# A layer kernel's attention stage: later value products, division moved to the output projection, maxima moved by transfers, loads moved to SyncE

## The chip, the cores and the metric

The kernel runs on one core of a Trainium2 chip, in one launch. The metric is the device time of that launch in microseconds. Before the change it is 2820.78 us, the median of three runs (2816.55 to 2822.61). Inputs and outputs are fp32.

## What is computed

One layer of a streaming encoder, for a prompt of 2048 frames and for eight streams of 16 new frames with 1024 cached frames each. Width 1024; half of the mixer is a convolution module of 512 channels, half is attention with 8 heads of 64. Cut to what matters:

```python
sh1, sc1, g1, sh2, sc2, g2 = split(silu(c) @ w_ada + b_ada)
h = rmsnorm(x, norm1_g) * (1 + sc1) + sh1
u_a, u_g, q, k, v, f = split(h @ w_in)
u = u_a * sigmoid(u_g)
q, k = rmsnorm(q, q_norm_g), rmsnorm(k, k_norm_g)        # per head
logf = log_sigmoid(f + b_f)
s = q @ k.T * 64 ** -0.5 + (cum_q[:, None] - cum_k[None, :])   # cum = cumsum(logf)
attn = softmax(where(k_pos <= q_pos, s, -1e30)) @ v
conv = silu(layernorm(depthwise_conv31(u) + conv_b) * ln_g + ln_b)
x = x + g1 * (concat(conv, attn) @ w_out)
h = rmsnorm(x, norm2_g) * (1 + sc2) + sh2
x = x + g2 * ((silu(h @ w_gate) * (h @ w_up)) @ w_down)
```

The outputs are x, the new keys, values, log forget values and convolution states.

## The kernel before, in words

fp32 products on TensorE are made of two parts: each operand is split into a rounded high part (a copy on ScalarE) and a low part (a subtraction on VectorE or GpSimd, `parts_of`, L1158), and a product is three matmuls: high by high, low by high, high by low.

The stages follow each other: the input projection of the gate, values and forget logits (`project_u_v`), queries and keys (`project_q_k`), attention (`attention`, L778), the output projection (`project_out`, L1178), and the feed-forward network (`ffn_up`, `ffn_down`). The depthwise convolution runs on VectorE beside the projections.

Attention over the prompt goes through 16 steps, `STEPS`: for each of four pairs of heads p, four blocks qb of 512 queries. A step has 8(qb + 1) pieces: for each block of 128 keys and each head of the pair a score product of 128 keys by up to 512 queries (`attend`, L954). A piece takes: two score matmuls (L973 with the keys' high and low parts, L977 with the rest of the operand), on the diagonal a third that adds the mask (L979); the exponential on ScalarE (L981); the split of its result into two parts `e` (L1160 and L1161, every third subtraction on GpSimd); and three value matmuls (L964) into one of two PSUM banks per head, `pv`. The value operand has a block of ones between the two heads' columns, so that the sums of the exponentials come out of the same products. Pieces wait in the list `waiting` and two are taken off it when it is too long; what is left at the end of the step is emptied there.

The softmax subtracts a maximum over keys. It is not found from the scores themselves: a separate product of the high parts (L934, with a mask at L936) gives approximate scores with queries on the partitions, VectorE reduces them (L937), and the result of a step is transposed on TensorE (L948) and written into 8 rows of the query operand `Q2` (L950), where a constant block mask `bm` puts each of the 8 values (head and block of 128 queries) into its own row and columns; rows of minus one in the key operand then subtract it within the score product. The maxima run ahead of the scores by `AHEAD` and `LEAD` pieces, and L974 orders a first score behind a maxima product further on.

Loads for attention: keys (L889, L891) and queries (L903, L927) are started from GpSimd's queue, values (L906) from SyncE's. There are six buffers for key blocks, four for `Q2`, two for `Q1`.

At the end of a step (L995 to L1006) ScalarE copies sums and values out of the two banks (four copies of 64 partitions), makes the reciprocal with Ln and Exp, VectorE refines it and multiplies (L1003 to L1005), and a DMA stores the block to `cat_d` in HBM, from which the output projection reads.

Beside the steps runs `background`: the norm of the convolution's output (`conv_norm`, five chunks, with two Newton rounds, L92, for an inverse root), then the attention of the eight streams (`sample_setup`, `sample_batch`), all through one PSUM bank `lane`. `weave` deals out turns of the steps, the maxima, the loads and the background by count; `nback` is the background's number of turns. A planner (`schedule_with_timeline_sim`) then sets the order on every engine and queue from priorities and its own estimate of times; `after` adds an order between two instructions of one engine without a semaphore.

The output projection takes six blocks of 360 or 368 frames (`HALVES`). In each it goes through eight chunks of 128 input channels, attention's four first (`OUT_ORDER`); it loads a chunk from `cat_d` (L1196), splits it and adds 24 matmuls into 8 accumulators, one PSUM bank each (L1144). Then each accumulator is scaled and added to x (L1152) in a buffer `x`, of which there are 20, and stored. The buffers of blocks 0 and 1 are kept for the second norm, which follows block 2 (L1226); those of later blocks come free when they are stored and squared.

## Time and profile before

The profile is of one execution, on the one core.

| what | us |
|---|---|
| runs, median (lowest to highest) | 2820.78 (2816.55 to 2822.61) |
| the profiled execution's own time | 2814.3 |
| its span, first to last instruction | 2812.5 |
| busy in the span: TensorE matmuls | 2718.6 |
| busy: VectorE / ScalarE / GpSimd | 2161.9 / 1428.7 / 503.9 |
| mean granted TensorE clock | 0.983 |

Engines are called PE (TensorE matmul), PEld (its weight loads), DVE (VectorE), ACT (ScalarE), POOL (GpSimd) and SP (SyncE, which here only starts DMAs). L12 is line 12 of the kernel before. A name such as `e<-ef,e` says what an instruction writes and reads, by the program's names. Matmuls overlap in the pipeline and their ends are modelled, so a busy PE is not a PE at its peak. Who ended a wait is inferred from semaphores. Attention lies at about 600 to 1205 us, the output projection at 1200 to 1410, the feed-forward network after it.

### The profile page before, as it was taken

The numbers are of one execution on the slowest core, as the hardware profiler recorded it, in microseconds if no ns is written. First come the engines' busy times: TensorE is split into PE (matmuls) and PEld (weight loads), VectorE is DVE, ScalarE is ACT, GpSimd is POOL, SyncE is SP. The second block draws the span as 40 slices with busy tenths as digits, with TensorE's granted clock in tenths as the row PEclk, the third lists the DMA queues.
The fourth block names the chain that finished last, engine by engine and source line by source line (L and its number), as shares of the span: only waits on it lengthen the run. The fifth ranks groups of instructions, "written<-read, shape, count | busy, mean of one in ns | idle before, by whom it ended". The sixth has DMA issues, their size and how long they took to land. (4 is left out here: it accounts for less than half of the span.)

```text
span 2812.5 us, 48566 instructions
## 1 busy us (share of the span) xinstructions
PE 2718.6 (97%) x16536; PEld 2515.7 (89%) x16536; DVE 2161.9 (77%) x4235; ACT 1428.7 (51%) x2812; POOL 503.9 (18%) x685
## 2 busy tenths in 40 slices
PE   7999999999989999999999999999999999999999
PEld 6999988866667777698999989999999999999999
DVE  2798898989888787546397989877887778666765
ACT  4443323357776777744354446444554446555552
POOL 3454411243333222214201110000000000000000
PEclk9999999979999999999999999999999999999999
DMA  8753657673334766365576869866786769788883
GB/s 325 249 192 107 191 209 267 182 204 109 101 95 128 203 179 189 130 215 179 181 259 209 294 215 308 268 221 218 233 287 214 226 190 319 244 284 257 271 255 116
DMA packets 389960, 599.24 MB, mean 213 GB/s; under 512 B 47136, under 2 KB 250048, under 8 KB 387664
## 3 DMA queue, kind: packets, MB, share of 16 engines
q1 hardware_dynamic: 375248, 570.73, 62.8%
q0 software_dynamic: 14464, 25.42, 3.9%
q8 instruction: 130, 2.13, 0.3%
q14 instruction: 118, 0.97, 0.1%
HBM read 421.97 MB, written 174.08 MB: 212 GB/s over the span
## 5 line engine op out<-in xcount | busy, mean ns | idle before, releaser
L1456 PE MATMUL z<-rT,rW 128*128 128x360 f32 (+1 forms) x8316 | 1383.3, 328 | 5.5 <-ACT rW L1160 1.4
L1456 PEld LDWEIGHTS z<-rT,rW 128*128 128x128 f32 x8316 | 1378.7, 188 | 8.1 <-ACT rW L1160 2.4
L1160 ACT ACTIVATE rW<-rR 128x512 fp32r<-128x512 f32 x714 | 434.4, 617 | 386.8 <-PE z L1456 272.1
L1161 DVE TENSOR_TENSOR rW<-rR,rW 128x512 fp32r<-128x512 f32 x714 | 479.5, 676 | 154.5 <-ACT rW L1160 151.3
L700 DVE SCALAR_TENSOR_TENSOR cv<-cu,cpar,cv 128x384 f32<-128x384 f32 x580 | 311.6, 614 | 2.8 <-ACT cv L698 2.8
L964 PE MATMUL pv<-e,V 128*128 128x512 f32 (+3 forms) x960 | 268.9, 388 | 14.1 <-DVE e L1161 6.3
L964 PEld LDWEIGHTS pv<-e,V 128*128 128x128 f32 x960 | 167.9, 194 | 71.7 <-DVE e L1161 14.6
L937 DVE TENSOR_REDUCE M<-mx 128x1 f32<-128x512 f32 (+2 forms) x320 | 188.7, 603 | 50.2 <-PE mx L934 31.7
L981 ACT ACTIVATE ef<-s 128x512 f32<-128x512 f32 (+3 forms) x320 | 167.1, 532 | 116.7 <-PE s L979 47.1
L512 PE MATMUL z<-hqx,wqh 128*128 128x384 f32 (+1 forms) x768 | 196.6, 333 | 1.0 <-DVE logf L347 1.0
L1160 ACT ACTIVATE rT<-traw 128x360 fp32r<-128x360 f32 (+1 forms) x315 | 149.1, 501 | 91.7 <-DMA traw<-gt_d 62.9
L1161 DVE TENSOR_TENSOR rT<-traw,rT 128x360 fp32r<-128x360 f32 (+1 forms) x315 | 157.6, 531 | 45.0 <-ACT rT L1160 44.7
L1161 POOL TENSOR_TENSOR e<-ef,e 128x512 fp32r<-128x512 f32 (+3 forms) x106 | 127.2, 1200 | 347.4 <-ACT e L1160 180.7
L1160 ACT ACTIVATE e<-ef 128x512 fp32r<-128x512 f32 (+3 forms) x320 | 175.5, 567 | 4.0
L1161 DVE TENSOR_TENSOR e<-ef,e 128x512 fp32r<-128x512 f32 (+3 forms) x214 | 149.1, 704 | 35.4 <-ACT e L1160 34.4
L512 PEld LDWEIGHTS z<-hqx,wqh 128*128 128x128 f32 x768 | 135.7, 188 | 18.9 <-issue 15.3
L934 PE MATMUL mx<-K,Q 96*128 96x512 f32 (+2 forms) x320 | 134.3, 427 | 17.5 <-DVE M L937 11.3
L1144 PE MATMUL acc<-ch,woh 128*128 128x360 f32 (+1 forms) x384 | 127.4, 333 | 10.0 <-ACT ch L1160 4.6
L1384 DVE TENSOR_TENSOR rR<-rR 128x512 f32<-128x512 f32 (+1 forms) x136 | 93.4, 707 | 50.9 <-DMA rR<-w_down 44.1
L973 PE MATMUL s<-Q,K 128*128 128x512 f32 (+3 forms) x320 | 125.8, 393 | 3.4 <-ACT ef L981 3.4
L1144 PE MATMUL acc<-ch,wol 128*128 128x360 f32 (+1 forms) x384 | 126.9, 331 | 0.0
L512 PE MATMUL z<-hqx,wql 128*128 128x384 f32 (+1 forms) x384 | 126.4, 329 | 0.0
(306 smaller groups left out, 3935.4 us busy)
## 6 DMA issues: line engine op xcount, KB each, us to landing
rR<-sup_d SPq DMA_DIRECT2D x176, 256.0 KB
rR<-w_gate SPq DMA_DIRECT2D x132, 256.0 KB
traw<-gt_d SPq DMA_DIRECT2D x154, 180.0 KB
rR<-w_down SPq DMA_DIRECT2D x104, 256.0 KB
rR<-sdn_d SPq DMA_DIRECT2D x96, 256.0 KB
rR<-w_up SPq DMA_DIRECT2D x88, 256.0 KB
sup_d<-rR SPq DMA_DIRECT2D x88, 256.0 KB
wa<-w_ada SPq DMA_DIRECT2D x16, 1024.0 KB
```

The source lines that it names most:

```text
L512: nc.tensor.matmul(z[:, :n], w[:, m], x[:, :n], start=(c == 0 and k == 0), stop=(c == CB - 1 and k == 2))
L700: self.pin(nc.vector.scalar_tensor_tensor(dst, src, w, acc[i], ALU.mult, ALU.add))
L934: self.mx.append(nc.tensor.matmul(mx[:, :w], Q2[0:AUX, h, j * P:(j + 1) * P], K2[kb][0:AUX, h, :w], start=True, stop=not diag))
L937: nc.vector.tensor_reduce(M[:, i, kb:kb + 1], mx[:, :w], AX.X, ALU.max)
L964: nc.tensor.matmul(z[h][:, off:], V[kt // 4][:, v, kt % 4, h:h + 2, :].rearrange("p b c -> p (b c)"), e[:, x, off:], start=(kt == 0 and i ...
L973: first = nc.tensor.matmul(s[:, off:], K1[kb][:, h, sl], Q1[:, h, off:], start=True, stop=False)
L981: self.last_piece = nc.scalar.activation(ef[:, off:], s[:, off:], AF.Exp)
L1144: self.nc.tensor.matmul(z[:, :n], w[:, m], y, start=(first and i == 0 and k == 0), stop=(last and i == len(terms) - 1 and k == 2))
L1160: copy = self.nc.scalar.activation(hi, raw, AF.Copy)
L1161: engine.tensor_tensor(lo, raw, f32(hi), ALU.subtract)
L1384: nc.vector.tensor_tensor(t, x, y, op)
L1456: nc.tensor.matmul(z, W[:, x, m], t[:, y, :w], start=(k == 0 and i == 0), stop=(k == n - 1 and i == 2))
```

## The change

Value products: the list of waiting pieces now belongs to the layer and not to the step. A piece's products are taken off one at a time when more than five wait (three while only five buffers `e` exist), and are not emptied at a step's end, so the last ones of a step are made in the next. Each piece's first value matmul is ordered behind the last score matmul issued (`self.last_s`); so are the lane's matmuls (`behind`).

End of a step: ScalarE copies each of the two banks whole (`zc`), a DMA stores one row of sums per head to `sum_d`, another the undivided values to `cat_d`. A turn of the next step (`inverses`) loads the sums as 128 partitions of 8, VectorE takes the reciprocal, and a DMA stores them to `inv_d`. The output projection loads, for each of attention's chunks, two broadcast rows of `inv_d` and multiplies on VectorE before it splits. The buffers `x` become 18.

Maxima: the 8 transposed rows are copied to SBUF and moved by eight DMAs, 128 values each, into one row of `Q2`; the key operand has one row of minus one in place of eight; `bm` goes.

Loads: keys and queries are started from SyncE, and the value staging buffer has a tag of its own. The lane's keys, bias rows and new keys are loaded a chunk or a stream ahead, the set-up of the streams is spread over turns, the norm waits two turns for its input, and `nback` counts the turns anew. The two Newton rounds of the query/key norm and of the convolution's norm become one. The lead of the maxima may grow to 10 pieces in place of 8.

```diff
-            newton_rsqrt(nc, y, zp.tile([P, NB], F32, tag="t", name="rt", bufs=1)[:, :n], v, 2, self.pin)
+            newton_rsqrt(nc, y, zp.tile([P, NB], F32, tag="t", name="rt", bufs=1)[:, :n], v, 1, self.pin)
...
         nc.sync.dma_start(y[:, :, :n], self.y_d[:, :, t0:t0 + n])
+        yield
+        yield
...
-        newton_rsqrt(nc, r, sp.tile([P, 512], F32, tag="cm", name="ct")[:, :n], v, 2)
+        newton_rsqrt(nc, r, sp.tile([P, 512], F32, tag="cm", name="ct")[:, :n], v, 1)
...
-        for k, r, v in (("v", slice(AUX, AUX + 8), -1.0), ("t", slice(HD, HD + 2), 1.0)):
+        for k, r, v in (("v", slice(AUX, AUX + 1), -1.0), ("t", slice(HD, HD + 2), 1.0)):
...
-        nback, done, units, scored = 15 + 5 * 7 + 1 + 8 * 11, 0, 0, AHEAD
+        nback, done, units, scored = 15 + 5 * 9 + 12 + 8 * 11, 0, 0, AHEAD
...
+            else:
+                parts.append((self.inverses(*STEPS[n - 1]), 4))
...
-            nc.gpsimd.dma_start(K2[0:HD + 2], rows[HD:])
+            nc.sync.dma_start(f32(K2[0:HD + 2]), rows[HD:])
...
-            nc.gpsimd.dma_start(k1, rows[0:P])
+            nc.sync.dma_start(f32(k1), rows[0:P])
...
-        nc.gpsimd.dma_start(Q1, self.q_d[2 * p:2 * p + 2, :, t].rearrange("h r t -> r h t"))
+        nc.sync.dma_start(f32(Q1), self.q_d[2 * p:2 * p + 2, :, t].rearrange("h r t -> r h t"))
...
-        raw = self.awk.tile([P, 4, P], F32, tag="rs", name="vraw", bufs=1)
+        raw = self.awk.tile([P, 4, P], F32, tag="vr", name="vraw", bufs=1)
...
-            nc.gpsimd.dma_start(Q2[0:HD], self.q_d[2 * p:2 * p + 2, 0:HD, t].rearrange("h r t -> r h t"))
+            nc.sync.dma_start(f32(Q2[0:HD]), self.q_d[2 * p:2 * p + 2, 0:HD, t].rearrange("h r t -> r h t"))
...
-        for h in range(2):
-            nc.vector.tensor_tensor(Q2[r, h, :].rearrange("r (j q) -> r j q", j=4),
-                                    pz[r, :].unsqueeze(1).broadcast_to([8, 4, P]),
-                                    self.bm[r, h, :].unsqueeze(2).broadcast_to([8, 4, P]), ALU.mult)
+        m = self.lp.tile([P, P], F32R, tag="mrow", name="mrow", bufs=1)
+        nc.vector.tensor_copy(m[r], pz[r])
+        for i in range(8):
+            nc.sync.dma_start(f32(Q2[AUX:AUX + 1, i // 4, i % 4 * P:(i % 4 + 1) * P]), f32(m[AUX + i:AUX + i + 1]))
...
-                at = min(self.nscore + AHEAD + min(self.nscore // 6, 8), len(self.mx) - 1)
+                at = min(self.nscore + AHEAD + min(self.nscore // 5, 10), len(self.mx) - 1)
...
-                waiting.append((kt, h, off, e))
-                if h and len(waiting) > len(self.eslots) - 3:
-                    value(*waiting.pop(0))
-                    value(*waiting.pop(0))
+                self.waiting.append((value, kt, h, off, e))
+                while len(self.waiting) > min(len(self.eslots) - 2, 5):
+                    self.next_value()
                 yield
-        for w in waiting:
-            value(*w)
-
-        pvs, sm = (wk.tile([P, 512], F32, tag=k, name=k, bufs=1) for k in ("pvs", "sm"))
-        for h in range(2):
-            o, x = slice(HD * h, HD * h + HD), slice(HD - HD * h, P - HD * h)
-            nc.scalar.copy(sm[o], z[h][x])
-            nc.scalar.copy(pvs[o], z[h][o])
-        r = wk.tile([P, 512], F32, tag="rs", name="rs", bufs=1)
-        nc.scalar.activation(r, sm, AF.Ln)
-        self.last_exp = nc.scalar.activation(r, r, AF.Exp, scale=-1.0)
-        nc.vector.tensor_tensor(sm, sm, r, ALU.mult)
-        nc.vector.scalar_tensor_tensor(sm, sm, 2.0, r, ALU.subtract, ALU.mult)
-        nc.vector.scalar_tensor_tensor(pvs, pvs, -1.0, sm, ALU.mult, ALU.mult)
-        self.last_store = nc.sync.dma_start(self.cat_d[:, 4 + p, qb * 512:(qb + 1) * 512], pvs)
+        if n + 1 == len(STEPS):
+            while self.waiting:
+                self.next_value()
+    def end_of_step(self, p, qb, h, z):
+        if h == 0:
+            self.zc = self.awk.tile([P, 2, 512], F32, tag="zc", name="zc", bufs=1)
+        t = slice(qb * 512, qb * 512 + 512)
+        self.last_exp = self.nc.scalar.copy(self.zc[:, h], z)
+        o, x = slice(HD * h, HD * h + HD), HD - HD * h
+        self.nc.sync.dma_start(self.sum_d[2 * p + h:2 * p + h + 1, t], self.zc[x:x + 1, h])
+        self.last_store = self.nc.sync.dma_start(self.cat_d[o, 4 + p, t], self.zc[o, h])
+    def inverses(self, p, qb):
...
+        r = self.awk.tile([P, 2, 4], F32, tag="inv", name="inv")
+        nc.sync.dma_start(r, self.sum_d[2 * p:2 * p + 2, t].rearrange("h (a c) -> a h c", c=4))
+        yield
+        nc.vector.reciprocal(r, r)
+        nc.sync.dma_start(self.inv_d[2 * p:2 * p + 2, t].rearrange("h (a c) -> a h c", c=4), r)
...
+            if c < 2:
+                self.next_keys(2 * b + c + 2)
+            else:
+                self.next_bias(b + 1)
...
+                else:
+                    inv = cp.tile([P, NW], F32, tag="ci", name="ci", bufs=2)[:, :n]
+                    for h in range(2):
+                        load = nc.sync.dma_start(inv[HD * h:HD * h + HD], self.inv_d[2 * (c - 4) + h:2 * (c - 4) + h + 1, b0:b1].broadcast_to([HD, n]))
...
+                    nc.vector.tensor_tensor(raw, raw, inv, ALU.mult)
...
-                x = sp.tile([P, NW], F32, tag="x", name="xo", bufs=20)
+                x = sp.tile([P, NW], F32, tag="x", name="xo", bufs=18)
```

More of the change, by code (lines that the diff above doesn't have):

```diff
@@ L715, in channel_mean @@
             for j in range(4):
-                nc.tensor.matmul(pm[32 * j:32 * j + 32, :n], self.ones[:, 0:32], src[j], start=True, stop=True,
+                self.behind(nc.tensor.matmul)(pm[32 * j:32 * j + 32, :n], self.ones[:, 0:32], src[j], start=True, stop=True,
                                  tile_position=(0, 32 * j))
@@ L782, in attention @@
         self.R.close()
-        self.split3 = 0
+        self.split3, self.turn, self.waiting, self.last_s = 0, 0, [], None
         self.Wout = {}
@@ L824, in attention @@
         drain(back)
+        drain(self.inverses(*STEPS[-1]))
         for g in range(NP):
@@ L875, in background @@
         self.smc = self.after_attention.enter_context(self.pool(name="smc", bufs=2))
-        self.sample_setup(bank)
-        yield
+        yield from self.sample_setup(bank)
         for b in range(NS):
@@ L957, in attend @@
         Q1, Q2 = self.Q1.pop(n), self.Q2[n % 4]
-        z = [self.bank("tr", "pv") for _ in range(2)]
         nkt = 4 * qb + 4
-        waiting = []
+        z = []
         def value(kt, h, off, e):
+            if kt == 0:
+                z.append(self.bank("tr", "pv"))
             for i, (v, x) in enumerate(((0, 0), (0, 1), (1, 0))):
-                nc.tensor.matmul(z[h][:, off:], V[kt // 4][:, v, kt % 4, h:h + 2, :].rearrange("p b c -> p (b c)"), e[:, x, off:],
-                                 start=(kt == 0 and i == 0), stop=(kt == nkt - 1 and i == 2))
+                product = nc.tensor.matmul(z[h][:, off:], V[kt // 4][:, v, kt % 4, h:h + 2, :].rearrange("p b c -> p (b c)"), e[:, x, off:],
+                                           start=(kt == 0 and i == 0), stop=(kt == nkt - 1 and i == 2))
+                if i == 0:
+                    self.after(product, self.last_s)
+            if kt == nkt - 1:
+                self.end_of_step(p, qb, h, z[h])
         for kt in range(nkt):
@@ new lines, in inverses, with behind, issue @@
+    def inverses(self, p, qb):
+        nc = self.nc
+        t = slice(qb * 512, qb * 512 + 512)
+        yield
+        yield
+        r = self.awk.tile([P, 2, 4], F32, tag="inv", name="inv")
+        nc.sync.dma_start(r, self.sum_d[2 * p:2 * p + 2, t].rearrange("h (a c) -> a h c", c=4))
+        yield
+        nc.vector.reciprocal(r, r)
+        nc.sync.dma_start(self.inv_d[2 * p:2 * p + 2, t].rearrange("h (a c) -> a h c", c=4), r)
+    def behind(self, op):
+        def issue(*args, **kw):
+            ins = op(*args, **kw)
+            self.after(ins, self.last_s)
+            return ins
+        return issue
@@ L1029, in sample_setup @@
         for kt in range(8):
-            nc.tensor.matmul(pt[:n, 2 * kt:2 * kt + 2], lf[:, kt, :], self.ones[:, 0:2], start=True, stop=True)
+            self.behind(nc.tensor.matmul)(pt[:n, 2 * kt:2 * kt + 2], lf[:, kt, :], self.ones[:, 0:2], start=True, stop=True)
         suf = sm.tile([P, 8], F32, name="suf")
@@ L1037, in sample_setup @@
             for i in range(4):
-                nc.tensor.matmul(pb[:n, i, :], lf[:, 4 * b + i, :], tri, start=True, stop=True)
+                self.behind(nc.tensor.matmul)(pb[:n, i, :], lf[:, 4 * b + i, :], tri, start=True, stop=True)
             nc.vector.tensor_tensor(
@@ L1632, in host_layout @@
                             for w in range(2)], 1))
-    bm = np.zeros((P, 2, 4), np.float32)
-    for h in range(2):
-        for j in range(4):
-            bm[AUX + 4 * h + j, h, j] = 1
-    r["bm"] = bm
     r["sel"] = np.concatenate([
```

65 lines of the change are left out of this document (46 added, 19 removed).

## The prediction

> **What bounds the kernel now.** I read the page first, then stretches, then who waited for whom, then groups, then single places in order of time.
>
> ```profile
> span 2812.5 us, 48566 instructions
> PE 2718.6 (97%) x16536; PEld 2515.7 (89%) x16536; DVE 2161.9 (77%) x4235; ACT 1428.7 (51%) x2812; POOL 503.9 (18%) x685
> ```
>
> Over the whole span TensorE (PE) looks full, but the change works almost entirely in the attention stage, so I cut the span there. Columns: stretch and its length, busy us of PE, PE weight load, DVE, ACT, POOL (with instructions), granted clock, DMA share, GB/s.
>
> ```profile
> 600.00:640.00 40.00, 36.23 (x104) 23.01 (x104) 32.61 (x62) 16.82 (x41) 18.33 (x22) 0.58 0.75 206
> 640.00:930.00 290.00, 264.94 (x1239) 192.87 (x1239) 243.12 (x418) 211.23 (x423) 93.60 (x91) 0.97 0.41 111
> 930.00:1070.00 140.00, 133.29 (x967) 103.06 (x968) 112.58 (x194) 102.34 (x202) 35.83 (x35) 0.98 0.70 190
> 1070.00:1205.00 135.00, 125.51 (x881) 94.20 (x880) 90.93 (x159) 105.02 (x212) 30.23 (x27) 0.96 0.47 154
> 1300.00:1350.00 50.00, 43.79 (x263) 41.76 (x262) 31.95 (x61) 20.76 (x41) 20.30 (x20) 1.00 0.69 228
> 1410.00:2812.00 1402.00, 1387.57 (x8365) 1383.76 (x8363) 1100.88 (x2134) 684.17 (x1336) 41.28 (x34) 0.99 0.76 244
> ```
>
> From 1410 on (the feed-forward network) weight loads fill 1383.76 of 1402 us: nothing there is touched or can be won. Attention is 600 to 1205: its four stretches leave PE idle for 3.8 + 25.1 + 6.7 + 9.5 = 45 us, and a busy PE there is not a dense one: weight loads fill 66% of 640 to 930 (192.87 / 290), 74% of 930 to 1070 and 70% of 1070 to 1205. In 640 to 930 DVE is busy 84%, the most of any stage; in 930 to 1070 it is 80%, and PE is then 95% busy. So PE and DVE hold each other up. The waits of that stage say so (columns: who waited for whom, us in total, times, longest; the first seven PE from 600 to 1205, the last two DVE from 640 to 930):
>
> ```profile
> PE mx L934 <- DVE M L937: 11.3, 15, 1.5
> PE pv L964 <- DVE e L1161: 6.3, 13, 1.1
> PE pv L964 <- POOL e L1161: 3.6, 7, 1.2
> PE pv L964 <- ACT e L1160: 3.6, 6, 1.2
> PE lane L1073 <- DVE S L1075: 4.1, 1, 4.1
> PE mx L934 <- DMA Q<-q_d: 2.8, 1, 2.8
> PE lane L716 <- DMA cy<-y_d: 2.6, 2, 2.2
> DVE M L937 <- PE mx L934: 16.9, 21, 2.0
> DVE M L937 <- PE mx L936: 14.3, 13, 3.9
> ```
>
> PE waits for DVE's row maxima and for the split exponentials (DVE, POOL, ACT), and DVE waits 31 us for PE's next maxima product: a loop with both sides late in turn, no single long stall.
>
> The Trainium skill, "Trainium Kernel Development and Optimization", section Performance Expectations, calls matmul busy time a bad measure because matmuls are pipelined, and the busy share of weight loads a good one. Read by the matmul row, 640 to 930 could give 25 us at the very most and rival 1 below would be impossible; read by the rule, 28 and more are open. The trace sides with the rule as far as it goes: the PE that is 91% busy here does its weight loads at two thirds of the rate of 1410 on.
>
> **The change part by part.** Columns below: line, engine, operation, shapes, count | busy us, mean ns | idle before.
>
> ```profile
> L950 DVE TENSOR_TENSOR Q<-pz,bm 8x512 fp32r<-8x512 f32 x32 | 20.9, 692 | 0.7 <-PE pz L948 0.2
> L1003 DVE TENSOR_TENSOR sm<-sm,rs 128x512 f32<-128x512 f32 x16 | 12.8, 799 | 0.0
> L1004 DVE SCALAR_TENSOR_TENSOR sm<-sm,rs 128x512 f32<-128x512 f32 x16 | 13.4, 840 | 0.1
> L1005 DVE SCALAR_TENSOR_TENSOR pvs<-pvs,sm 128x512 f32<-128x512 f32 x16 | 13.2, 823 | 0.1
> L94 DVE SCALAR_TENSOR_TENSOR ct<-cr 128x512 f32<-128x512 f32 (+1 forms) x10 | 7.7, 766 | 0.1
> L95 DVE TENSOR_TENSOR ct<-ct,cvar 128x512 f32<-128x512 f32 (+1 forms) x10 | 7.6, 761 | 0.1
> L96 DVE SCALAR_TENSOR_TENSOR cr<-ct,cr 128x512 f32<-128x512 f32 (+1 forms) x10 | 7.3, 730 | 0.0
> L999 ACT COPY pvs<-pv 64x512 f32<-64x512 f32 x32 | 18.6, 580 | 0.7
> L1117 DVE COPY catS<-lane x16: 206/222/228, 966.3 to 1197.5; 64x64 f32<-64x64 f32 x16
> ```
>
> DVE work taken off attention: the maxima's spreading 20.9; the division after each of 16 steps 12.8 + 13.4 + 13.2 = 39.4; one of two Newton rounds of the convolution's norm, half of 22.6 = 11.3. Added: 16 copies of 8 rows and 16 reciprocals of 8 elements a row, at 0.22 (the small copy L1117) 7 us. Net 71.6 - 7 = 65 us of DVE off 605. ACT loses two of four end-of-step copies (18.6, as L999) and both 128x512 Ln and Exp, and is nowhere the last to finish; I price that at nothing: PE covers it. The Newton round in the query/key norm is hidden by PE, which is saturated there; without cover it would be worth 3 operations a block.
>
> By stretch. 640 to 930 holds 8 of the 16 spreadings (11.1 us), 7 step ends (17.2) and all five norms: 39.6 less 3.2 added = 36 off 243. If DVE keeps its 84% share the stretch shrinks to 207 / 0.84 = 247, a gain of 43; if PE can only become as dense as in 930 to 1070 (74% weight loads) it shrinks to 192.87 / 0.736 = 262, a gain of 28; if the loop of maxima is unmoved and only the value waits on DVE and POOL go, 6.3 + 3.6 = 10. I take **28**, since PE's density is the tighter. 930 to 1070 frees 4 spreadings and 4 ends, 14 us, but PE is idle 6.7 only: I take **4** (0 to 7). 1070 to 1205: 9.5 idle, part of it at the very end where the last step's values are emptied at once: **5** (0 to 10). 600 to 640 runs at a granted 0.58; two spreadings fall there, and I book nothing for the clock: **2** (0 to 5).
>
> "Five pieces behind" within a step is nearly what stands: the list is emptied by two when it has over five, so values already trail by four to six. New is that the last five cross into the next step, and that each value, and each lane matmul, is ordered behind the last score. Its worth is inside the numbers above; by itself it is bounded by the pv waits, 6.3 + 3.6 + 3.6 = 13.5 us, and below by minus 9, if each of 16 steps now waits for a 0.58 copy to free a bank. The lanes' earlier loads (keys, bias rows, the norm's input) are bounded alike by the lane waits, 4.1 + 2.6 = 6.7 us; their empty turns are made up by the larger count of background turns, 160 for 139.
>
> **Queues.** POOL loses 64 loads and what stood behind them; SP gains them, and 128 transfers of 512 bytes, 32 + 16 stores and loads for sums and inverses, 16 more stores to cat.
>
> ```profile
> L891 POOL DMA_DIRECT2D K<-k_d x16 | 11.7, 734 | 22.3 <-PE s L977 13.8 <-PE z L512 4.6 <-PE s L973 3.9
> L903 POOL DMA_DIRECT2D Q<-q_d x16 | 11.8, 739 | 30.5 <-PE s L979 25.6 <-PE z L512 2.7 <-DVE M L937 2.0
> L557 SPq DMA_DIRECT2D q_d<-qp x48: 574/589/1000, 414.0 to 647.5; - x48
> L646 SPq DMA_DIRECT2D k_d<-lft x32: 263/293/916, 165.9 to 372.8; - x32
> SPq L906 <- DVE sm L1004: 166.2, 12, 30.5
> SPq L1057 <- PE mx L934: 16.5, 2, 13.9
> ```
>
> SP's time for it: 64 x 0.59 (like q_d, two heads a transfer) + 128 x 0.29 (4 KB, the smallest with a count) + 64 x 0.34 or less = at most 97 us in 605; it also loses its longest wait, 166 us for a buffer shared with the division. So SP has the time (a wait at its head is idle time, and costs only what stands ready behind it). What is new is the order: the loads' waits for finished scores (25.6 + 13.8 + 3.9 = 43 us on POOL, in front of POOL's third of the splits) now stand in front of stores, lanes and maxima on SP. POOL's end of it is worth at most the 3.6 us of pv waits on POOL. SP's end costs between nothing (each wait ends before its follower is needed) and 43 us (each is passed on to PE whole); I take **4**, near the low end, because PE's only wait for such loads today is 2.8 us.
>
> The maxima's chain gets longer. Today (DVE, then PE, in order of time; start, length):
>
> ```profile
> 704.50 1.31 DVE L950 TENSOR_TENSOR Q<-pz,bm 8x512 fp32r<-8x512 f32 x2
> ```
>
> ```profile
> 711.81 0.40 PE L977 MATMUL s<-Q,K 128*128 128x512 f32 x1
> ```
>
> and a landing of 4 KB (issues on POOL's queue, KB each, us to landing):
>
> ```profile
> n1T<-n1T POOLq DMA_DIRECT2D x1, 4.0 KB, 5.6
> ```
>
> They are ready at 705.8 and first read at 711.8: 6.0 us of slack before the first of the four steps with four key blocks (shorter steps follow longer leads). New: 0.22 copy + 8 x 0.29 issues + landing. For a landing the nearest rows are 5.6 (4 KB on POOL's queue) and the 3.2 from issue to use on SP's queue below, so 5.7 to 8.1 against today's 1.3 and 6.0 + 1.3 = 7.3 allowed; the limit of the lead rises from 8 to 10 pieces, some 3 us. Late by minus 5 to plus 1, four times, more if SP is held. I take **3** in all (0 to 12). The Trainium skill, "DMA: Bandwidth & Descriptors", Rules for kernel authors, speaks against such transfers: under 64 KB one pays mostly overhead. By the roughly 2 us that its section on the anatomy of a DMA gives each, the chain would be 4.5 us and the cost nothing.
>
> **Output projection.** 24 multiplies of 128x360 on DVE (about 0.52 each, by the x4 row below) and 48 loads lie under PE; DVE is busy 32 of 50 there at most. Uncovered they would be 12.5 us. But x gets 18 buffers for 20. Blocks 0 and 1 hold 16, so block 2's eight pieces rotate through 4 now and 2 then:
>
> ```profile
> 1303.71 2.08 DVE L1152 SCALAR_TENSOR_TENSOR xo<-acc,mod,xo 128x360 f32<-128x360 f32 x4
> ...
> 1310.09 0.59 DVE L1152 SCALAR_TENSOR_TENSOR xo<-acc,mod,xo 128x360 f32<-128x360 f32 x1 [2.12 <-DMA xo<-xT]
> ```
>
> ```profile
> 1306.87 3.25 SPq L1211 DMA_DIRECT2D xo<-xT  x4
> PE acc L1144 <- DVE xo L1152: 4.3, 5, 1.9
> ```
>
> A piece's buffer comes round in 1310.1 - 1303.7 = 6.4 us. Four pieces, one round, and four more spread as SP's four loads are (3.25) end some 9.7 after the start; two at a time need three rounds, 19.2 + 2 x 0.52 = 20.2. The last accumulator comes free 10.5 later, and PE, which waits 4.3 for them now, has nothing else. I take **8** lost (0 if buffers are found elsewhere, 14 with a dip of the clock). At the end of attention the last sums make four transfers before use, but block 0 needs only inverses of first query blocks, long done: nothing.
>
> **Sum.** 28 + 4 + 5 + 2 = 39 gained, 4 + 3 + 8 = 15 lost, net 24. The profiled execution took 2814.3 us, 1.8 over its span; it becomes 2790. It is 6.5 below the median of the runs, 2820.78; 24 off that gives **2797**.
>
> **Rivals.** (1) DVE alone sets 640 to 930: gain 43, and 7 + 10 + 5 in the others, 65 with the transfers covered and 8 lost in the projection: 57 net, 2764. For it: DVE 84% against PE's 66% of weight loads. Against: DVE waits 31 us for PE. (2) The gain stays out, because values already trail enough and the mx-M loop is what binds: 10 + 0 + 2 + 2 less 15, 2822, no difference. For it: the largest PE wait is mx on M, 11.3, which no edit touches directly. (3) Slower: SP, in order, is held in front of the maxima and the next step's operands. It has waits of 13.9 already at L1057. If the 43 us of waits moved from POOL reach PE whole and the tight steps lose 12, that is 55 + 8 lost against 39: 2845. It decides from about 31 us of such waits in place of my 7. Against: the loads have four and six buffers.
>
> **Chances and range.** Forecast 0.57, rival 1 0.14, rival 2 0.12, rival 3 0.17. The forecast's own range is 2780 to 2812 (first stretch 15 to 36, projection 4 to 12, partly together). Reaching into both sides of rivals 1 and 3 until two in ten are left out: 2765 to 2826. Some 0.2%, 5.6 us, is what a measurement of this kernel can tell from no change. Faster: 0.57 + 0.14 = 0.71; same: rival 2 less a point, 0.11; slower: 0.17 + that point = 0.18.
>
> **What would show it.** Attention's end (1205 now) some 31 us earlier; weight loads in its first half at 72% or more; no L950, DVE about 65 us lighter; POOL's splits no longer behind loads; PE waiting for xo about 12 us in block 2 of the projection, with three pauses of about 6 us on DVE. Wrong if scores wait for DMA into Q or mx for Q and K by more than 10 us in total (rival 3), if DVE's share stays 84% with the stretch 40 us shorter (rival 1), or if mx still waits for M by 11 us and the stretch is unmoved (rival 2).

## The result, and the profile after

The changed kernel takes 2839.11 us (median of 5 runs, 2830.91 to 2843.73); the kernel before, run beside it, 2817.02 (2816.55 to 2822.61). The ratio is 1.007 with a 95% interval of 1.0049 to 1.0091: 22 us slower. The forecast was 2797, with a range of 2765 to 2826.

The profiled execution after took 2837.18. Its page begins:

```profile
span 2835.4 us, 48858 instructions
PE 2716.6 (96%) x16536; PEld 2524.2 (89%) x16536; DVE 2095.4 (74%) x4178; ACT 1401.7 (49%) x2748; POOL 460.2 (16%) x621
```

VectorE is 66.5 us lighter (2161.9 before), as forecast (65). The span grew by 22.9 all the same. To see where, take the first and last start of three groups of matmuls: the last block of z (end of the query, key and value projections), pv (value products of attention) and acc (output projection). Columns of these rows: count, duration in ns (least/median/most), first and last start. Before:

```profile
L512 PE MATMUL z<-hqx,wqh x768: 274/334/446, 346.2 to 596.3; 128*128 128x384 f32 x160, 128*128 128x256 f32 x32
L964 PE MATMUL pv<-e,V x960: 220/393/796, 631.3 to 1197.6; 128*128 128x512 f32 x138, 128*128 128x256 f32 x25, 128*128 128x384 f32 x15, 128*128 128x128 f32 x14
L1144 PE MATMUL acc<-ch,woh x384: 321/329/674, 1200.5 to 1406.7; 128*128 128x360 f32 x128, 128*128 128x368 f32 x64
L1144 PE MATMUL acc<-cl,woh x384: 321/327/412, 1204.8 to 1407.0; 128*128 128x360 f32 x128, 128*128 128x368 f32 x64
```

After:

```profile
L514 PE MATMUL z<-hqx,wqh x768: 274/334/446, 343.0 to 592.2; 128*128 128x384 f32 x160, 128*128 128x256 f32 x32
L971 PE MATMUL pv<-e,V x960: 219/392/796, 621.5 to 1177.4; 128*128 128x512 f32 x140, 128*128 128x256 f32 x20, 128*128 128x384 f32 x16, 128*128 128x128 f32 x16
L1206 PE MATMUL acc<-ch,woh x384: 321/330/677, 1191.0 to 1428.7; 128*128 128x360 f32 x128, 128*128 128x368 f32 x64
L1206 PE MATMUL acc<-cl,woh x384: 321/327/595, 1195.9 to 1429.0; 128*128 128x360 f32 x128, 128*128 128x368 f32 x64
```

| us | until attention | attention (last z to last pv) | gap (last pv to first acc) | projection (first to last acc) | rest of the span | span |
|---|---|---|---|---|---|---|
| before | 596.3 | 601.3 | 2.9 | 206.5 | 1405.5 | 2812.5 |
| after | 592.2 | 585.2 | 13.6 | 238.0 | 1406.4 | 2835.4 |
| difference | -4.1 | -16.1 | +10.7 | +31.5 | +0.9 | +22.9 |

So 20 us were won up to the end of attention, of the 32 that the forecast had there (39 gained, less 4 and 3), and 42 were lost right behind it. The same four lengths are read in this way for every run below. The length until attention differs between profiles of equal code by some 5 us (592.1 to 596.8 among the runs below that leave it as changed), so its 4.1 us say little.

**Attention.** The stretches of after, with the columns of the prediction:

```profile
640.00:930.00 290.00, 265.01 (x1264) 199.78 (x1263) 213.30 (x388) 199.16 (x395) 65.73 (x56) 0.94 0.41 123
930.00:1070.00 140.00, 136.20 (x975) 104.22 (x974) 98.71 (x187) 95.44 (x190) 30.64 (x27) 0.99 0.64 186
1070.00:1179.00 109.00, 103.60 (x790) 78.34 (x789) 64.81 (x117) 84.04 (x169) 25.21 (x22) 1.00 0.45 143
1179.00:1192.00 13.00, 1.02 (x3) 1.02 (x4) 1.76 (x4) 1.28 (x2) 0.00 (x0) 0.61 0.58 117
```

In 640 to 930, where the forecast had 28 of its 39 us, VectorE went from 243.1 to 213.3 busy, and TensorE is as busy as before (264.9, now 265.0), at a granted clock of 0.94 for 0.97. Weight loads fill 69%, not 72. The value products alone in that stretch say the same: 473 of them before, 471 after (first row before, second after).

```profile
640.00:930.00 290.00, 136.20 (x473) 0.97 0.41 111
```

```profile
640.00:930.00 290.00, 129.56 (x471) 0.94 0.41 123
```

So the 16 us do not come from the stretch in which the forecast had its 28. In 600 to 640 there are 34 value products for 17, at a granted clock of 0.72 for 0.58, and after 930 the changed kernel needs 247 us for its remaining 455 products, where the kernel before needed 268 for 470.

The waits of after in attention (596 to 1160: PE, then VectorE and SyncE):

```profile
PE mx L939 <- DVE M L942: 14.2, 16, 3.1
PE mx L939 <- DVE mrow L955: 2.4, 2, 2.2
PE s L984 <- DMA Q<-q_d: 2.3, 1, 2.3
```

```profile
DVE inv L1030 <- DMA inv<-sum_d: 20.8, 9, 4.3
```

```profile
SPq L1028 <- DMA sum_d<-zc: 25.0, 16, 3.7
```

The value waits on the split exponentials (13.5 us before) are gone. New is that VectorE stands 20.8 us in front of the tiny reciprocals, in order, with row maxima and splits queued behind it. SyncE stands 25.0 us until the stored sums have landed, because the load that follows reads them. The Trainium skill, "DMA: Bandwidth & Descriptors", Rules for kernel authors, demands that wait: a transfer that reads what an earlier one wrote must wait for its completion. The trace shows how long SyncE stands for it: the 25.0 us.

**The gap.** The same execution in order of time (start, length, what; in brackets idle time and releaser):

```profile
1177.39 1.07 ACT L1016 COPY zc<-pv 128x512 f32<-128x512 f32 x2 [2.37 <-PE pv L971]
1178.01 0.24 SPq L1018 DMA_DIRECT2D sum_d<-zc  x1
...
1180.57 0.39 SPq L1028 DMA_DIRECT2D inv<-sum_d  x1
...
1182.43 0.20 DVE L1030 RECIPROCAL inv<-inv 128x8 f32<-128x8 f32 x1 [4.11 <-DMA inv<-sum_d]
1182.66 0.37 SPq L1031 DMA_DIRECT2D inv_d<-inv  x1
1183.07 0.47 SPq L1258 DMA_DIRECT2D cr<-cat_d  x1
1183.64 1.11 SPq L1266 DMA_DIRECT2D ci<-inv_d  x2
...
1189.84 0.54 DVE L1269 TENSOR_TENSOR cr<-cr,ci 128x368 f32<-128x368 f32 x1 [7.21 <-DMA ci<-inv_d]
...
1190.98 0.68 PE L1206 MATMUL acc<-ch,woh 128*128 128x368 f32 x1 [13.15 <-ACT ch L1222]
```

The last step's sums go out and come back (1178.0 to 1182.4), the inverse goes out, and only then, behind it on the same queue, come the first loads of the projection. The first multiply waits until 1189.8 for them. The projection needs none of the last step's inverses in its first block; it waits for their place in the queue. That its loads could go earlier is read from the order of this trace, and from div_back below.

**The projection.** PE's waits in it:

```profile
PE acc L1206 <- ACT ch L1222: 20.1, 4, 13.2
PE acc L1206 <- DVE xo L1214: 10.9, 5, 4.5
PE acc L1206 <- ACT cr L1262: 4.2, 1, 4.2
```

The first row holds the gap's 13.2. And the stretch of the projection alone, first before, then after:

```profile
1200.00:1407.00 207.00, 198.38 (x1183) 195.91 (x1184) 95.27 (x185) 83.34 (x160) 56.13 (x55) 0.99 0.59 193
```

```profile
1191.00:1429.00 238.00, 211.87 (x1183) 207.32 (x1184) 101.99 (x205) 81.09 (x156) 55.78 (x55) 0.93 0.59 183
```

The same matmuls keep PE busy 13.5 us longer, at a granted clock of 0.93 for 0.99, and PE is idle for 26 us instead of 9. So 17.5 of the 31.5 us are idle time, and the rest goes with the lower clock that stands beside the stalls; why the clock is lower is not shown.

### The profile page after: what moved, and what is told of

Its sections match the earlier page's. It is cut to its first block, busy times and chain, and to the rows that moved or that the text cites. A ratio compares the mean times of both kernels' runs of the same rounds, so it can differ in the third digit from the quotient of the medians.

```text
span 2835.4 us, 48858 instructions
## 1 busy us (share of the span) xinstructions
PE 2716.6 (96%) x16536; PEld 2524.2 (89%) x16536; DVE 2095.4 (74%) x4178; ACT 1401.7 (49%) x2748; POOL 460.2 (16%) x621
## 5 line engine op out<-in xcount | busy, mean ns | idle before, releaser
L971 PE MATMUL pv<-e,V 128*128 128x512 f32 (+2 forms) x960 | 260.5, 381 | 0.6 <-ACT e L1222 0.6
L1223 DVE TENSOR_TENSOR e<-ef,e 128x512 fp32r<-128x512 f32 (+3 forms) x214 | 140.4, 660 | 40.5 <-ACT e L1222 38.5
L1206 PE MATMUL acc<-ch,woh 128*128 128x360 f32 (+1 forms) x384 | 133.2, 349 | 36.5 <-ACT ch L1222 20.1
L939 PE MATMUL mx<-K,Q 96*128 96x512 f32 (+2 forms) x320 | 137.2, 435 | 17.9 <-DVE M L942 14.2
```

Source lines behind the costliest of these rows:

```text
L939: self.mx.append(nc.tensor.matmul(mx[:, :w], Q2[0:AUX, h, j * P:(j + 1) * P], K2[kb][0:AUX, h, :w], start=True, stop=not diag))
L971: product = nc.tensor.matmul(z[h][:, off:], V[kt // 4][:, v, kt % 4, h:h + 2, :].rearrange("p b c -> p (b c)"), e[:, x, off:], start=(kt = ...
L1206: self.nc.tensor.matmul(z[:, :n], w[:, m], y, start=(first and i == 0 and k == 0), stop=(last and i == len(terms) - 1 and k == 2))
L1223: engine.tensor_tensor(lo, raw, f32(hi), ALU.subtract)
```

## Experiments

All numbers in one place. Ratio: to the runs of the kernel before on the same chip, with its 95% interval; lengths in us from each run's profile.

| run | median us | ratio | attention | gap | projection |
|---|---|---|---|---|---|
| div_back | 2789.88 | 0.9904 (0.9884-0.9923) | 572.2 | 2.9 | 208.8 |
| no_inverse | 2790.78 | 0.9903 (0.9885-0.9921) | 569.1 | 3.5 | 216.6 |
| ci_pool | 2837.34 | 1.0068 (1.0044-1.0091) | 583.0 | 14.1 | 235.3 |
| before_x18 | 2827.19 | 1.0032 (1.0021-1.0043) | 601.9 | 2.9 | 220.0 |
| inv_late | 2843.61 | 1.0084 (1.0055-1.0113) | 583.9 | 13.4 | 239.2 |
| inv_behind | 2831.35 | 1.0045 (1.0030-1.0061) | 577.6 | 13.0 | 238.2 |
| sums_behind_pool | 2830.35 | 1.0042 (1.0019-1.0065) | 575.1 | 10.2 | 241.1 |
| mul_const | 2817.94 | 1.0001 (0.9990-1.0011) | 584.2 | 12.2 | 221.4 |
| ci_unread | 2830.00 | 1.0051 (1.0034-1.0067) | 584.6 | 12.6 | 231.4 |
| ci_3 | 2828.28 | 1.0052 (1.0032-1.0071) | 584.0 | 13.7 | 229.8 |
| last_divides | 2834.71 | 1.0061 (1.0042-1.0080) | 584.4 | 13.9 | 235.3 |
| before_proj | 2846.96 | 1.0095 (1.0069-1.0122) | 591.4 | 12.8 | 243.1 |
| div_loads_pool | 2784.33 | 0.9879 (0.9864-0.9894) | 574.0 | 2.9 | 206.0 |
| div_step_end | 2803.89 | 0.9947 (0.9930-0.9965) | 589.3 | 4.9 | 206.3 |
| div_maxima_dve | 2798.91 | 0.9925 (0.9906-0.9945) | 582.4 | 4.7 | 209.1 |
| div_recip_pool | 2806.03 | 0.9954 (0.9936-0.9971) | 595.6 | 3.6 | 206.2 |
| div_back_b | 2790.26 | 0.9896 (0.9875-0.9918) | 575.5 | 2.9 | 206.4 |
| div_loads_pool_b | 2785.04 | 0.9880 (0.9859-0.9901) | 576.2 | 2.9 | 204.5 |

How far profiles of equal code differ can be read off it: attention by some 3 us (div_back twice; the six profiles with attention as changed, after and last_divides among them, lie between 583.0 and 585.2), the projection by up to 6 (235.3 to 241.1 in the runs that leave it as changed).

**Is it the division's new place?** div_back undoes that part, and gives x its two buffers back:

```
     def end_of_step(self, p, qb, h, z):      # x bufs 18 -> 20, no inverses, no ci
-        self.last_exp = self.nc.scalar.copy(self.zc[:, h], z)
-        (stores of the sum row and of cat)
+        nc.scalar.copy(sm[o], z[x]); nc.scalar.copy(pvs[o], z[o])
+        if h == 0: return
+        (Ln, Exp, three operations on VectorE, one store, as in the kernel before)
```

> The changed kernel, but each step divides in attention as before (two more copies, Ln, Exp and three operations on VectorE a step; one store to cat; no sums and inverses through HBM, x with 20 buffers). Theory A (the loss is the division's new place): the output projection shrinks from 238 us to 207-211, the wait between attention and projection from 13.3 to 2.6-4 us; attention gives back 0 to 13 us of its 16 for the 39 us of VectorE work; 2797 to 2812 us. Theory B (SyncE's order in attention is the loss, the prediction's third rival): no change from 2839, or above 2830. Theory C (the loss is the two missing buffers of x alone): 2825 to 2831, the wait of 13.3 stays.

It is, by 49 us, of which x's two buffers are some 10 (below): 2789.9, faster than both kernels. Gap and projection are back at 2.9 and 208.8. Against the expectation attention did not give anything back: VectorE is busy 439.3 us in it instead of 413.3, and it is 10 to 13 us *shorter* than in the changed kernel (the two profiles of div_back).

no_inverse leaves sums, inverses and multiplies out altogether (x stays at 18):

```
-        self.nc.sync.dma_start(self.sum_d[...], self.zc[x:x + 1, h])
-        (the calls of inverses(); the ci loads and the multiply)
```

> The changed kernel with the sums, the inverses, their loads and the multiplies left out; cat goes undivided into the projection (so the output is another); x keeps 18 buffers. Theory A: wait at the start 2.6-4 us, projection 207-218, attention unmoved; 2795 to 2810. Theory C (18 buffers of x): only the 10.7 us at the start go, the projection stays above 230; 2825 to 2831. Against the run with the division back it gives the price of dividing in attention.

Attention, expected unmoved, is 569: dividing in it costs 3 to 7 us, dividing through HBM 16. The time, 2790.8, lies 4 us below the range expected. The projection is still 8 longer than in div_back, which is x's buffers. These are priced alone by before_x18:

```
-                x = sp.tile([P, NW], F32, tag="x", name="xo", bufs=20)
+                x = sp.tile([P, NW], F32, tag="x", name="xo", bufs=18)
```

> The kernel before with 18 instead of 20 buffers of x in the output projection, nothing else. The prediction's term: 8 us slower (0 to 14), all of it in the projection's third block: 2825. Theory A (the inverses make the loss): 0 to 4 us, 2817 to 2821.

9.8 us, all in the projection (13.5 longer in the profile). PE waits 9.9 us for x instead of 4.3, and 6.2 of this at the end of the third block, where the prediction had it (2.9 before). These waits are less than half of the 13.5: PE is also busy 7.3 us longer, at a granted clock of 0.95 for 0.99. In 1300 to 1330 VectorE makes its eight additions in the time below (first to last start), standing before x:

```profile
PE acc L1144 <- DVE xo L1152: 9.9, 6, 2.8
```

```profile
L1152 DVE SCALAR_TENSOR_TENSOR xo<-acc,mod,xo x8: 586/592/596, 1305.2 to 1323.1; 128x360 f32<-128x360 f32 x8
its engine sat idle before it (us, times) until:
  DMA xo<-xT: 10.8, 4
```

17.9 + 0.6 us for the eight: the forecast was 20.2.

before_proj puts the new place of the division, alone, into the kernel before (copies, sums, inverses(), ci, x at 18, as in the change):

> The kernel before with that one part of the change alone: sums and inverses through HBM, the projection divides, x with 18 buffers. Theory A (this part is the loss, wherever it is put): the difference between the changed kernel and its version with the division back is 49 us, so 2817 + 35 to 55 = 2852 to 2872, projection 228 to 240, wait ahead of it 9 to 15. The prediction's step (39.4 us of VectorE's work taken off attention bring most of 28 + 4 + 5, and 8 are lost to x): 2790 to 2810.

29.7 us slower, 5 short of theory A's range. Gap and projection lose 46.5 there (42 in the changed kernel), but attention *wins* 10 there, where in the changed kernel the same part loses 10 to 13. So what 39 us less on VectorE is worth depends on the order around it; why it won there was not followed further.

**What in attention costs the 16 us?** inv_late takes the inverse a step after its load:

```
+        self.invert()                     # the step before's
         r = self.awk.tile([P, 2, 4], F32, tag="inv", name="inv")
         nc.sync.dma_start(r, self.sum_d[...])
-        yield
-        nc.vector.reciprocal(r, r)
-        nc.sync.dma_start(self.inv_d[...], r)
+        self.loaded = r, p, t
```

> The changed kernel, but VectorE takes the inverse of a step's sums one step later, when their load has long landed; the loads of sums stay where they are on SyncE. Theory A (attention's 585 us against 569 without inverses is VectorE standing in order before the reciprocal, 20.8 us in 9 waits for the load): attention 569 to 575, 2823 to 2830. Theory B (SyncE standing before the load of sums until their store has landed, 25.0 us in 16 waits): attention stays 582 to 587, 2834 to 2842.

Nothing followed: VectorE still stood 20.1 us, since the order on the engine is a planner's, which moved the reciprocal forward. inv_behind forces it:

```
-            self.nc.vector.reciprocal(r, r)
+            self.after(self.nc.vector.reciprocal(r, r), self.last_s)
```

> As the run before with the inverse taken one step later, whose edit had not moved the wait (VectorE still stood 20.1 us before the reciprocal, since the planner put it forward): now the reciprocal is also ordered behind the last score issued a step later. Theory A (VectorE standing before the reciprocal is what attention loses to the inverses): that wait falls under 5 us, attention 569 to 576, 2822 to 2832. Theory B (SyncE standing before the load of sums): the wait goes, but attention stays 581 to 587, 2834 to 2846.

Now the wait is gone from attention; the rows of the inverses over the whole run (count, ns, first and last start; idle before):

```profile
L1037 DVE RECIPROCAL inv<-inv x16: 182/192/203, 681.1 to 1178.2; 128x8 f32<-128x8 f32 x16
...
its engine sat idle before it (us, times) until:
  DMA inv<-sum_d: 3.8, 1
```

Attention falls from 585.2 to 577.6, 1.6 us above theory A's range and clear of theory B's; the kernel is 7.8 us faster than the changed one. sums_behind_pool takes SyncE's part away as well:

```
-        nc.sync.dma_start(r, self.sum_d[...])          # and the store of inv_d
+        nc.gpsimd.dma_start(r, self.sum_d[...])
```

> As inv_behind, with the loads of sums and the stores of inverses on GpSimd's queue, so that SyncE stands before neither. If SyncE's standing there is the rest of attention's loss: attention 568 to 573 (577.8 in inv_behind, 569.1 without inverses), 2820 to 2828. If it is not: 576 to 582, 2827 to 2836.

575.1: between both expectations, 2.5 less, which is within what equal code differs. So of the 16 us, VectorE's standing is some 7.6; SyncE's is not told apart from nothing; 6 remain unassigned.

**What in the projection?** ci_pool, the loads of inverses off SyncE's queue:

```
-                        load = nc.sync.dma_start(inv[...], self.inv_d[...])
-                        if bi < 2:
-                            self.queued(load)
+                        nc.gpsimd.dma_start(inv[...], self.inv_d[...])
```

> The changed kernel with the 48 loads of inverses on GpSimd's queue and out of the ordered list of loads, so that nothing on SyncE's queue waits behind them; two buffers as before. Theory A1 (SyncE is held behind the inverses' buffers and so brings cat too late): the stalls between blocks of 29 us fall to 9-15, projection 210-222, 2811 to 2825 (the wait of 13 us at the start may stay). Theory A2 (the inverses themselves arrive too late through two buffers, whoever issues): projection 232-240, 2833 to 2841.

No difference, but the waiting moved: VectorE stands 7.0 us before the inverses (21.5 in the changed kernel), and PE waits 19.0 us for x (10.9). So SyncE's standing behind the inverses' buffers does not set the time. mul_const multiplies by ones and loads nothing:

```
-                    (inv tile, two loads)
-                    nc.vector.tensor_tensor(raw, raw, inv, ALU.mult)
+                    nc.vector.tensor_tensor(raw, raw, self.one_nw[:, :n], ALU.mult)
```

> The changed kernel, sums and inverses made in attention as there, but the projection multiplies by a constant tile of ones in place of the inverses and doesn't load them (so the output is another); x keeps 18 buffers. Theory A (the loads and their wait through two buffers make the projection's loss): projection 216 to 221 as without inverses, wait ahead of it 4 to 8 us; 2807 to 2817. Theory B (the multiply itself, on VectorE ahead of each split, makes it): projection 228 to 238, 2822 to 2834.

221.4: the loads cost 16.6 of the projection's 31.5; the multiply 4.8 (against no_inverse), which is less than equal code differs by. The gap stays, against 4 to 8 expected: 12.2. ci_unread keeps the loads and takes only the waiting away (it multiplies by ones, too):

> The changed kernel with the 48 loads of inverses in their place and order, but the multiply takes a constant one instead of what they bring (so the output is another). If the waiting for them is the cost: projection 220 to 227 (221.7 without the loads), 2816 to 2826. If the 48 transfers themselves are (their issue on SyncE, their share of the DMA engines): projection 232 to 240, 2830 to 2840.

231.4, between the expectations and nearer the second. Some 6.6 would be the waiting, which is not clear of the 6 by which equal code differs (the intervals of the ratios overlap, too); 10.0 the presence of 48 more transfers, and here the ratios are apart (1.0051 and 1.0001). PE's waits put it on x: 15.6 us, against 9.3 in mul_const. Since PE waits for x with the loads on the other queue as well (ci_pool), how the transfers delay it stays open. ci_3 gives a third buffer (`name="ci", bufs=3`; the rows of w_out get two):

> The changed kernel with three buffers of inverses instead of two; two instead of three buffers for the rows of w_out that are loaded in the first block make the room. If the rotation through two buffers is a good part of the loss: projection 226 to 233, 2826 to 2834. If not: 235 to 241, 2834 to 2843.

229.8, so the rotation through two buffers is up to 8 us of it. This and the 6.6 above are two readings of the same waiting, not two shares.

**And the gap?** last_divides lets the last step alone divide on the chip, with ones stored as its inverses:

```
+        if (p, qb) == STEPS[-1]:
+            return self.last_division(p, qb, h, z)
-        drain(self.inverses(*STEPS[-1]))
```

> The changed kernel, but the last step alone divides on the chip (its inverses are stored as ones beforehand), so that no chain of sums and inverses stands between attention and projection; the projection's loads of inverses stay. The chain alone explains 13.3 us down to 3-4 if the first loads of inverses land as fast as cat; 7 to 9 if they take the 6 us from issue to use that they took there. Total 2828 to 2834.

A miss on both counts: 13.9. SyncE now stood before the store of cat until VectorE had divided (5.6 us), and the planner again put the projection's first loads behind it, at 1188.2. In div_back four of these loads stand ahead of that store:

```profile
1166.42 1.86 SPq L1263 DMA_DIRECT2D cr<-cat_d  x4
...
1172.22 0.33 SPq L1024 DMA_DIRECT2D cat_d<-pvs  x1
```

mul_const, which loads no inverses, keeps its gap of 12.2 and has its first loads behind the last store of inverses. So the gap goes with the order of the first loads against the last step's last transfer, whatever that transfer is. No run moves this order alone; it is read from these traces.

**What did bring attention its time?** By div_back against the kernel before it is 26 to 29 us. Three parts of the change undone one by one, in the version with the division back. The 64 loads on GpSimd's queue:

```
-            nc.sync.dma_start(f32(k1), rows[0:P])      # and K2, Q1, Q2
+            nc.gpsimd.dma_start(k1, rows[0:P])
```

> The version with the division back in attention (2789.9), with the 64 loads of keys and queries on GpSimd's queue again as in the kernel before. If moving them to SyncE brings a good part of attention's 29 us (splits on GpSimd no longer behind loads that wait for scores): attention 580 to 592, 2797 to 2810. If it brings nothing, as the prediction had it (at most 3.6 won, 4 lost): 569 to 576, 2786 to 2794.

5.5 us faster, which neither theory had. Measured again, side by side on one chip:

> The division in attention and the 64 loads on GpSimd's queue once more, beside the version with the loads on SyncE on the same chip. If moving the loads to SyncE costs some us: 2782 to 2787. If the difference was the chips': within 2 us of the other.

> The division in attention and the loads on SyncE once more: 2786 to 2792 if the move costs 3 to 7 us; within 2 us of the other if not.

5.2 us once more, the two intervals overlapping. Taken together, the eight runs with the loads on GpSimd lie between 2781.9 and 2787.9, the nine with SyncE between 2782.4 and 2796.6. The profiles do not show the difference (spans of 2783.5 and 2783.8 against 2782.6 and 2780.7), so its place stays open. This is the fastest version: 0.988 of the kernel before.

Values that do not cross the end of a step:

```
-        if n + 1 == len(STEPS):
-            while self.waiting:
-                self.next_value()
+        while self.waiting:
+            self.next_value()
```

> The version with the division back in attention (2789.9), but every step empties its list of waiting value products at its own end, so that none crosses into the next step. If the crossing brings a good part of attention's 29 us: attention 582 to 595, 2800 to 2812. The prediction bounded it by the value waits of 13.5 us from above and minus 9 from below: between 2781 and 2803. If it brings nothing: 570 to 575, 2788 to 2793.

14 us slower; attention 589.3. The crossing is the largest gain among the parts that were undone. It is not idle time that it saves. Attention from the last z to the last pv, first div_back, then div_step_end:

```profile
594.40:1166.60 572.20, 536.27 (x3175) 403.37 (x3174) 439.34 (x785) 432.46 (x867) 140.56 (x121) 0.96 0.49 150
592.60:1181.90 589.30, 551.78 (x3177) 406.19 (x3175) 446.60 (x787) 431.65 (x868) 139.35 (x121) 0.96 0.47 146
```

Of the 17 us, 15.5 are the same matmuls keeping PE busy for longer at the same granted clock, and 1.6 are idle. So a list of PE's waits could not have priced it; what makes the matmuls closer is not shown. Maxima spread on VectorE:

```
-        (copy of 8 rows, eight transfers)
+        nc.vector.tensor_tensor(Q2[r, h, :]..., pz..., self.bm..., ALU.mult)     # two
```

> The version with the division back in attention (2789.9), with the maxima spread by two multiplies on VectorE (20.9 us in all) as in the kernel before, instead of one copy and eight transfers a step. If VectorE's busy time sets attention: 17 us more work at its share of 0.8 is 14 to 20 us more, 2803 to 2810. If the transfers hide it but it is no bound: 0 to 4, 2788 to 2794. If the transfers themselves delay the scores: 3 to 8 faster, 2782 to 2787.

9 us slower, between the first two expectations; attention 582.4. Of PE's waits in attention the largest are:

```profile
PE mx L937 <- DVE M L940: 13.7, 18, 2.1
PE mx L937 <- DVE Q L953: 7.6, 9, 2.0
```

PE's next maxima stand behind the two multiplies for 7.6 us; behind the one short copy of div_back they don't. But in div_back they wait 18.3 us for M, for 13.7 here, so PE's idle time is only 1.5 us longer here (37.4 for 35.9), and 8.7 of the 10 us are again matmuls that keep PE busy for longer. That the length of VectorE's piece at this place counts would fit; it is not shown. Together the crossing and the maxima are 23 us; the other parts (the order behind the last score, the Newton rounds, the lane's earlier loads, the longer lead) were not undone alone.

**A cheaper division?** div_recip_pool, on top of the fastest version:

```
-        (Ln, Exp, three operations)
+        nc.vector.reciprocal(sm, sm)
+        nc.vector.tensor_tensor(pvs, pvs, sm, ALU.mult)
```

> The fastest version so far (division in attention, loads of keys and queries on GpSimd's queue, 2784.3), with one reciprocal of 128x512 on VectorE and one multiply a step in place of Ln, Exp and three operations. If the reciprocal takes about as long as the other operations of that size (0.8 us): 13 us less on VectorE, 2 us less on ScalarE a step; 0 to 6 faster, 2778 to 2785. If it takes several times that, it holds the maxima and splits behind it 16 times: 2790 to 2810.

21.7 us slower:

```profile
L1018 DVE RECIPROCAL sm<-sm 128x512 f32<-128x512 f32 x16 | 53.5, 3344 | 4.6 <-ACT sm L1014 4.6
```

## Why the prediction was wrong

By its own terms, measured in profiles (attention without the inverses: 569.1, from no_inverse, the one run in which VectorE has neither the division nor the inverses, as the forecast's 39 had it):

| term | forecast | measured |
|---|---|---|
| attention and ahead of it, without the inverses | -39 + 4 + 3 | -32.2 - 4.1 |
| inverses in attention | 0 (3.5 us of VectorE's work netted off) | +16.1 |
| "four transfers before use ... nothing" | 0 | +10.7 |
| multiplies and loads in the projection, "lie under PE" | 0 | +21.4 (4.8 + 16.6) |
| x 20 to 18 | +8 | +10.1 (no_inverse against before); +9.8 timed alone |
| rest | 0 | +0.9 |
| sum | -24 | +22.9 |

*The step that failed* is the pricing of the division's second half at nothing. Its cost was counted in busy time (16 reciprocals of 0.22 us, 24 multiplies of 0.52, 48 issues) and laid under PE, since VectorE had 18 of 50 us free there. The runs showed 16.1 us in attention, 10.7 in the gap and 21.4 in the projection in place of these zeros. In attention each reciprocal waits for a transfer on an engine that works in order, 20.8 us ahead of operations worth 3; ordering them later gives 7.6 back, and 6 are not assigned. In the projection some 6.6 are such waiting, 10.0 come with the 48 transfers being there at all, by a way that stays open, and 4.8 are the multiplies. The prediction looked for waits behind SyncE alone and did not ask what is queued behind VectorE's. At the end of attention it asked whether the last inverses are *needed* early, and not whether the loads that are needed stand *behind* them on the queue.

*The second failing* is inside a row that came out near, and by luck: -32 forecast up to the end of attention, -36.3 measured without the inverses, but by another sum. 36 us of VectorE's work off 640 to 930 were turned into 28 by a density of PE. In the changed kernel nothing of it came (471 value products for 473); part of this is the reciprocals' standing, for 481 fit in inv_behind. But the rate was too high as well. First no_inverse, then div_back:

```profile
640.00:930.00 290.00, 131.05 (x489) 0.96 0.43 126
640.00:930.00 290.00, 130.61 (x484) 0.97 0.41 125
```

VectorE is busy 217.5 us there in the first and 239.4 in the second, and the 22 us are worth 5 value products, some 3 us (an estimate, at 290 us for 484). The whole division, 39 us, costs attention 3 to 7; at the forecast's rate of 28 for 36 it would be 31. The maxima's 17 us brought 9, which is near that rate less the 3 for lateness. So what VectorE's work is worth depends on where it stands, and one rate for a stretch was wrong. The crossing of step ends, 14 us, had been bounded at 13.5 by PE's waits and hidden inside the 28; it came as busy time and not as waits. Rival 1 falls with this: VectorE's share in 640 to 930 is 74%, and the stretch holds no more value products than before.

*What held*: VectorE 65 lighter (66.5); x's buffers in size (8 forecast, 9.8 timed; eight additions 20.2, measured 18.5), though only half in kind: the forecast had it all as waiting in the third block and read the 4.3 us of waits before as lying there, where 2.9 do; alone, two buffers fewer brought 5.6 us more of waits and 7.3 more of busy time at a lower clock, and in the changed kernel only 3.1 of the 10.9 us of waits for xo stand at the end of that block; the maxima's chain late by 3 (2.4 us of waits on mrow), though an issue took 0.59 us on SyncE and not 0.29; the loads' move to SyncE a loss of 4 (about 5 timed, not seen in the profiles); splits on GpSimd no longer late.

*Rival 3* forecast the right sign and, at 2845, a nearer time, by another mechanism: SyncE holding scores and maxima in attention. Its own sign was over 10 us of scores and maxima waiting for Q and K; there are 2.5. The mechanism that was missing from the list, as far as it is shown, is the same in kind, an in-order engine standing before a transfer, at two other places: VectorE in attention and projection, and the queue at the seam between them. *Rival 2's* sign came true in the changed kernel: mx still waits 14.2 us for M, and 640 to 930 is unmoved. Its cause did not. Without the inverses mx waits 12.6 us for M, and 489 products fit in the stretch; what held it there was at least in part the standing before the reciprocals, and not that loop alone.

## What to carry to other kernels

Price an operation that reads a transfer by the time its engine will stand before it, with everything queued behind, and not by its busy time alone; here a round trip through HBM to save 39 us of VectorE's work cost some 40 us more than the division that it replaced. Price work on an engine by what leaves with it at its place: 39 us of VectorE's were worth 3 to 7 here. At the seam of two stages look at the order of the queue: which of the next stage's first loads are issued behind the last stage's last transfer, needed or not. And undo a change part by part even when it is slower as a whole: without the division's new place this one was worth 27 us, without the loads' move as well 33.

## What the hardware showed

A reciprocal on VectorE took 3.34 us for 128x512 against 0.20 for 128x8, some 6.2 ns for each further element of a row, where a product of 128x512 took 0.80. The Trainium skill, "VectorE: DVE Perf Modes", section First, the fixed hardware budget, gives the reciprocal a repeat count of 8; here it was about four times the product, and a division by Ln, Exp and three such operations (2.4 us of VectorE's time, in div_loads_pool) was cheaper.

A round trip of a few KB through HBM took some 4 us to be read (1178.0 to 1182.4), and 92 KB of one row spread to 64 partitions were used 6.2 us after the first of their two issues (1183.64 to 1189.84). The clock granted to the projection fell from 0.99 to 0.93 when PE's idle time in it rose from 9 to 26 us. It doesn't follow the idle time in proportion: without inverses (no_inverse), with 11 us idle, it was 0.94.

```profile
1165.00:1381.50 216.50, 205.92 (x1185) 203.66 (x1185) 91.33 (x182) 81.55 (x157) 56.44 (x55) 0.94 0.57 184
```
